# The two feed-forwards of a hybrid decoder layer: operands in a fixed order without POOL, two plain tiles, reads of products first, feeds a job sooner

## The chip, the cores and the metric

One core of a Trainium2 chip runs the whole layer as one program. The metric is the device time of the program in microseconds (us); the profile shows one execution of it, and the runs give a median. TensorE (PE) multiplies, VectorE (DVE), ScalarE (ACT) and GpSimd (POOL) work element by element, and SyncE (SP) issues the DMA transfers.

## What is computed

The reference is one layer of a decoder on 1024 tokens of width 1024, all in float32. The change touches the two feed-forwards (`D_FF` is 2816); the mixer between them and the last two lines stay.

```python
def swiglu(x, w_in, w_out):
    gate, up = jnp.split(x @ w_in, 2, axis=-1)
    return (jax.nn.silu(gate) * up) @ w_out

h = x
h = h + 0.5 * swiglu(rms_norm(h, ffn1_norm[i]), ffn1_w_in[i], ffn1_w_out[i])
h = h + hybrid_mixer(rms_norm(h, mix_norm[i]), ...)
h = h + 0.5 * swiglu(rms_norm(h, ffn2_norm[i]), ffn2_w_in[i], ffn2_w_out[i])
hn = rms_norm(h, ple_norm[i])
h = h + jax.nn.sigmoid(hn @ ple_w_gate[i]) * (p[i] @ ple_w_proj[i])
return rms_norm(h, final_norm)
```

`rms_norm(x, g)` divides by the root of the mean square and multiplies by the gain `g`. The kernel multiplies by the gain before the matmuls, and by the factor of the root, `R`, behind them.

## The kernel before

**Layout.** Activations lie transposed: eight tiles `h` of 128 channels x 1024 tokens. Each float32 operand is made of two parts for PE: ACT copies it into a rounded head, and DVE subtracts the head from the source, which leaves the rest. `part` (L282 ACT, L283 DVE) does that for an activation block of 128x512, `headrest` for a weight block, `split` for a whole 128x1024 tile. A product of two such operands takes three matmuls (head x head, head x rest, rest x head) of 512 columns.

**Seven products.** A job is one pair of output tiles times all its inputs. Both factors are cut into 2x2 blocks, and seven products of sums of blocks stand in for eight. `SEVEN = (1, 5, 6, 3, 7, 2, 4)` is the order of the products, called q = 0 to 6 in the loops. Three banks of PSUM hold them: products 1, 6, 7 and 4 add up in bank 0, 5 and 3 in bank 1, 2 has its own. A bank that takes another product must be read before that product is added to it; `done` reads it, on ACT or DVE. A job of four block pairs has 7 x 12 = 84 matmuls, one of three 63. The first job is plain, with eight products in four banks: 96 matmuls.

**Jobs.** A feed-forward has 22 jobs for the hidden layer (job 0 plain, 1 to 21 by sevens) and then 12 for the output: three windows of hidden tiles (`WINDOWS`), four jobs each (22 to 25, 26 to 29, 30 to 33; the last four are the short ones). 2784 matmuls in all.

**Operands of the hidden jobs.** `ffn` first goes through the eight tiles: square them, multiply by the gain in place (L324, DVE), make the plain blocks, and `ready` makes the sums of blocks on DVE and POOL (L308 to L311) and their parts. These are issued on engines without an order of their own: the compiler's planner orders them by simulated time. The sums of squares go to POOL and DVE (`squares`, L517, L519); the statistics are transposed on PE (`pstat`), reduced on DVE, raised to -1/2 on POOL, and spread by four matmuls with `ones` (`pr`), which ACT copies into `R`.

**Weights.** `load7` loads a job's blocks (two transfers of 512 KB, buffers `wr` for two jobs), `sums7` makes four sums on POOL (`ws`), `split7` makes the next head and rest; five buffers `w` let it run up to four products ahead (`AHEAD`). In `seven`, after the matmuls of a product:

```python
            self.split7()
            if q < 4:
                self.sums7(job + 1, q)
            if q == 3:
                self.load7()
            j.done(p, ps[at])
```

**Order.** `self.te`, `self.ve`, `self.ac` and `self.pl` (`_InOrder`) keep the instructions that go through them in the order of the program on their engine; `nc.vector` and the like are free, as are transfers on SP. `later(job, q, f)` runs `f` after product q of a job.

**Output jobs.** `hidden` gates the products and stores each hidden tile (`hid`), and `sums` stores sums of blocks of them (`ts`), with two of their four operations on POOL. For each window a `feed` loads blocks of `hid` and `ts` (256 KB each, buffers `b`, at most six asked ahead) and makes `part`s of them during the last job before the window and its first job. `bring` loads the residual tiles, two at a time (`hr`), and `added` adds the products to them. In the last window the result is squared again, and split (`take`) for the stage that follows.

Of the kernel before, what the change touches and what calls it, by code (L numbers as in the profile page):

```python
# [55 lines left out]
class Layer:  # L56
# [143 lines left out]
    def start(self, jobs):  # L200

        self.jobs = jobs
        self.loaded, self.ready, self.todo = 0, [], collections.defaultdict(list)
        self.next = (1, 0)
# [17 lines left out]
    def sums7(self, job, step):  # L222
# [10 lines left out]
        self.pl.tensor_tensor(j.w[p], x, y, op=op)  # L233
# [16 lines left out]
    def seven(self, job):  # L250
# [3 lines left out]
        for q, p in enumerate(SEVEN):  # L254
# [24 lines left out]
    def part(self, src, pool, tag, ac=None, eng=None):  # L279

        o = pool.tile([P, T], FR, tag=tag, name="xo")
        (ac or self.ac).activation(o[:, :512], src, AF.Copy)  # L282
        (eng or self.ve).tensor_tensor(o[:, 512:], src, F(o[:, :512]), op=ALU.subtract)  # L283
        return o

    def ffn(self, hs, gain, gain2, d, keep, pool, hp, xa, follow, beside=None):


        nc = self.nc
        lo, hi = slice(0, 512), slice(512, 1024)  # L290
        vx, ax, px = nc.vector, nc.scalar, nc.gpsimd
# [9 lines left out]
        plain, late = {}, []  # L301
        square, R, rs = self.squares(pool, False)

        def ready(kp):

            y1, y2 = hs[2 * kp], hs[2 * kp + 1]
            t1, t2, t3 = m(), m(), m()
            vx.tensor_tensor(t1, y1[:, hi], y1[:, lo], op=ALU.subtract)  # L308
            px.tensor_tensor(t3, y2[:, hi], y1[:, hi], op=ALU.subtract)
            vx.tensor_tensor(t2, y2[:, hi], t1, op=ALU.subtract)  # L310
            px.tensor_tensor(y2[:, lo], y2[:, lo], t2, op=ALU.subtract)  # L311
            for p, t in ((5, t1), (6, t2), (7, t3)):
                xs[p][kp] = self.part(t, *place(p), ax, vx)

            def four():
                xs[4][kp] = self.part(y2[:, lo], *place(4))
            self.later(1, kp, four)

        for kp in range(KP):
            for j in (2 * kp, 2 * kp + 1):  # L320
                square(j, hs[j])
                if keep is not None:
                    nc.sync.dma_start(keep[j], hs[j])
                vx.tensor_scalar(hs[j], hs[j], self.gains[:, gain + j:gain + j + 1], None, op0=ALU.mult)  # L324
                for p, h in (((1, lo), (0, hi)), ((2, lo), (3, hi)))[j % 2]:
                    o = plain[j, h.start] = self.part(hs[j][:, h], *place(p), ax, vx)
                    if p:
                        xs[p][kp] = o
            if kp:
                ready(kp - 1)  # L330
        ready(KP - 1)


# [9 lines left out]
        def feed(wi):  # L343
# [4 lines left out]
            for c in range(n):  # L348
                while todo and len(asked) < 6:
# [3 lines left out]
                    asked.append((t, p, i))  # L353
                t, p, i = asked.pop(0)
# [60 lines left out]
        for f in range(1, NF):  # L415
# [7 lines left out]
        w = self.jobs[0].w  # L423
        pp = {(a, h): self.psum([P, 512], F32, tag="d", name="pd") for a in range(2) for h in (0, 512)}
        for step in range(4):
            self.sums7(1, step)
        self.load7()
        self.split7()
        for kp in range(KP):
            ks = slice(kp * P, (kp + 1) * P)  # L430
            for i in range(2):
                for a in range(2):
                    for ww, halves in ((0, (0, 512)), (1, (0,))):
                        for h in (0, 512):
                            for v in halves:
                                self.te.matmul(pp[a, h], w[a + 1, i + 1][:, ww, ks], plain[2 * kp + i, h][:, v:v + 512],
                                               start=(kp == 0 and i == 0 and ww == 0 and v == 0),
                                               stop=(kp == KP - 1 and i == 1 and ww == 1))
        for _ in range(AHEAD - 1):
            self.split7()  # L440
        next(rs)
        self.later(1, 0, lambda: next(rs, None))

        def first():
            g = pool.tile([P, T], F32, tag="t", name="g")
            u = us[0] = hp.tile([P, T], F32, tag="h", name="u")
            for a, t in enumerate((g, u)):
                for h in (lo, hi):
                    self.ve.tensor_tensor(t[:, h], pp[a, h.start], R[:, h], op=ALU.mult)
            self.ac.activation(g, g, AF.Silu)  # L450
            self.ve.scalar_tensor_tensor(u, u, 0.5, g, op0=ALU.mult, op1=ALU.mult)
            nc.sync.dma_start(hid[0], u)
        self.later(1, 1, first)
# [4 lines left out]
        for job in range(1, len(self.jobs)):  # L458
# [4 lines left out]
            if out + 1 in (0, KP, 2 * KP):  # L463
                wi = (out + 1) // KP
                feeds, made, turn = feed(wi), 0, 0
                total, freed = 7 * (WINDOWS[wi][1] - WINDOWS[wi][0]), self.jobs[job].n // P
            if out == 2 * KP:
                square, Rn, rsn = self.squares(pool, True)
# [6 lines left out]
            for q in self.seven(job):  # L475
                if feeds is not None:
# [901 lines left out]
```

## Time and profile before

| what | value |
|---|---|
| median of 3 runs (lowest to highest) | 2762.5 us (2756.7 to 2762.56) |
| profiled execution | 2760.93 us |
| its span, first to last instruction | 2759.2 us |
| mean granted clock of PE | 0.975 |
| first feed-forward, then mixer, second feed-forward, end | 0 to 711, to 1928, to 2627, to 2759 us |

The profile is of one execution. Times in it count from the start of the span. An engine's busy time is the time in which it had an instruction running. A wait is given with its releaser, the work that ended last before the waiting instruction began. Matmuls overlap, so a run of them is read by its start, its length and its count.

### The profile page before, as it was taken

To read this page: it belongs to the slowest core of one execution; us is meant where nothing else is said; L and a number is where in the kernel's file an instruction comes from. 1 tells how busy PE (TensorE), PEld (TensorE's weight loads), DVE (VectorE), ACT (ScalarE), POOL (GpSimd) and SP (SyncE) were. 2 spreads that over 40 slices of the span, in tenths; PEclk is the share of its full clock that TensorE was granted. 3 is DMA by queue.
4 is the path that set the end of the run, shared out by engine and by line. 5 is a ranking of instruction groups with operands and counts; after the bars stand their busy time and mean duration, and the time that the engine had idled before them with its cause. 6 is when DMAs were issued, how large, how long until landed. Compare 5 with 4: busy or idle time off the path is not lost.

```text
span 2759.2 us, 33250 instructions
## 1 busy us (share of the span) xinstructions
PE 2598.9 (94%) x12022; PEld 2149.6 (78%) x12022; DVE 1806.6 (65%) x3138; ACT 1143.9 (41%) x1797; POOL 886.9 (32%) x599
## 2 busy tenths in 40 slices
PE   5999999999999999899999999999599999899897
PEld 3788887787788878788778877888488888788776
DVE  8555556777668999987255663232865555877776
ACT  4333334344455455523256662121443333443542
POOL 6455554422000240423222220110555555432300
PEclk9999999999999999999999999999799999999999
DMA  2243334444323233332432255332033233554322
GB/s 108 92 141 111 111 107 168 169 163 134 110 75 109 85 123 115 115 125 74 165 104 88 93 211 217 115 120 96 19 122 126 102 120 122 185 181 132 104 93 84
DMA packets 124068, 333.61 MB, mean 121 GB/s; under 512 B 13912, under 2 KB 34304, under 8 KB 123904
## 3 DMA queue, kind: packets, MB, share of 16 engines
q1 hardware_dynamic: 123904, 331.49, 34.7%
q8 instruction: 94, 1.54, 0.2%
q14 instruction: 70, 0.57, 0.1%
HBM read 226.55 MB, written 102.26 MB: 119 GB/s over the span
## 4 chain that ended last, share of the span: by engine, by line
PE 42%; DVE 4%; ACT 2%; DMA 2%; issue 1%; POOL 0%; DVEq 0%; POOLq 0%; SPq 0%; ACTq 0%
PE pd L1265 21%; PE pd L139 17%; DVE xo L283 1%; PE ptp L1195 1%; DMA b<-d_ts 1%; DMA a_l<-d_dq 0%; DVE xo L1265 0%; DVE a_l L1172 0%; DVE w L1265 0%; PE pqk L1153 0%; PE pv L1203 0%; DMA xh<-d_og 0%; PE pqk L1154 0%; PE pv L1204 0%; PE pqk L1156 0%
## 5 line engine op out<-in xcount | busy, mean ns | idle before, releaser
L1265 PE MATMUL pd<-xo,w 128*128 128x512 f32 x5568 | 1299.7, 395 | 89.2 <-DVE xo L283 34.8
L1265 PEld LDWEIGHTS pd<-xo,w 128*128 128x128 f32 x5568 | 1060.4, 191 | 327.2 <-DVE xo L283 41.1
L139 PE MATMUL pd<-xh,wh 128*128 128x512 f32 x1346 | 532.1, 397 | 12.4 <-DVE z L930 11.9
L139 PE MATMUL pd<-xl,wh 128*128 128x512 f32 x1346 | 530.9, 396 | 0.0
L139 PE MATMUL pd<-xh,wl 128*128 128x512 f32 x1346 | 453.5, 395 | 0.0
L1265 DVE TENSOR_TENSOR w<-wr,w 128x512 fp32r<-128x512 f32 (+1 forms) x272 | 231.0, 851 | 213.2 <-ACT w L1265 213.0
L139 PEld LDWEIGHTS pd<-xh,wh 128*128 128x128 f32 x1346 | 254.8, 190 | 67.4 <-DVE z L930 11.6
L139 PEld LDWEIGHTS pd<-xl,wh 128*128 128x128 f32 x1346 | 255.2, 190 | 51.9 <-issue 0.5
L139 PEld LDWEIGHTS pd<-xh,wl 128*128 128x128 f32 x1346 | 254.3, 190 | 52.9 <-issue 0.7
L118 DVE TENSOR_TENSOR wl<-wr,wh 128x1024 fp32r<-128x1024 f32 (+1 forms) x106 | 127.9, 1206 | 193.3 <-issue 96.6
L1265 ACT ACTIVATE w<-wr 128x512 fp32r<-128x512 f32 (+1 forms) x272 | 166.1, 614 | 192.7 <-PE pd L1265 140.3
L1265 POOL TENSOR_TENSOR g<-g,R 128x512 f32<-128x512 f32 x84 | 122.7, 1461 | 378.0 <-ACT g L1265 378.0
L1265 ACT ACTIVATE w<-ws 128x512 fp32r<-128x512 f32 (+1 forms) x198 | 122.4, 618 | 275.4 <-PE pd L1265 179.7
L117 ACT ACTIVATE wh<-wr 128x1024 fp32r<-128x1024 f32 (+1 forms) x106 | 101.7, 960 | 251.8 <-PE pd L139 236.0
L1265 POOL TENSOR_TENSOR ws<-wr 128x512 f32<-128x512 f32 (+1 forms) x66 | 104.5, 1583 | 249.5 <-DVE w L1265 143.0
L1265 DVE TENSOR_TENSOR hr<-hr,pd 128x512 f32<-128x512 f32 x168 | 114.8, 683 | 100.7 <-PE pd L1265 100.3
L1265 DVE TENSOR_TENSOR w<-ws,w 128x512 fp32r<-128x512 f32 (+1 forms) x198 | 138.8, 702 | 2.3 <-ACT w L1265 0.7
L1265 DVE TENSOR_TENSOR xo<-b,xo 128x512 fp32r<-128x512 f32 x154 | 124.2, 846 | 6.3 <-ACT xo L1265 6.2
L1265 ACT ACTIVATE g<-pd 128x512 f32<-128x512 f32 x84 | 50.3, 599 | 154.8 <-PE pd L1265 154.8
L999 POOL TENSOR_TENSOR g_e<-g_b 128x512 f32<-128x512 f32 x28 | 33.4, 1191 | 243.5 <-DVE g_b L973 182.2
L1265 POOL TENSOR_TENSOR ws<-wr,ws 128x512 f32<-128x512 f32 (+1 forms) x66 | 98.2, 1488 | 26.3 <-DVE w L1265 22.6
L1265 DVE TENSOR_SCALAR_CACHE_REDUCE k_junk<-sc,k_t 128x384 uint8<-128x384 f32 (+3 forms) x128 | 103.5, 809 | 3.0
(276 smaller groups left out, 3364.5 us busy)
## 6 DMA issues: line engine op xcount, KB each, us to landing
wr<-wm SPq DMA_DIRECT2D x54, 512.0 KB, 3.4
wr<-w1i SPq DMA_DIRECT2D x44, 512.0 KB, 4.1
d_hid<-u SPq DMA_DIRECT2D x44, 512.0 KB, 4.7
d_ts<-ts SPq DMA_DIRECT2D x44, 512.0 KB, 2.6
b<-d_ts SPq DMA_DIRECT2D x88, 256.0 KB, 4.0
wr<-w2i SPq DMA_DIRECT2D x44, 512.0 KB, 4.0
b<-d_hid SPq DMA_DIRECT2D x66, 256.0 KB, 4.7
wr<-w1o SPq DMA_DIRECT2D x16, 512.0 KB, 5.4
```

The source lines that it names most:

```text
L117: (ac or nc.scalar).activation(wh, raw, AF.Copy)
L118: (eng or self.weng).tensor_tensor(wl, raw, F(wh), op=ALU.subtract)
L139: te.matmul(ps[h], ww[:, ks], v[:, h * 512:h * 512 + 512], start=first and ww is wh and v is xh, stop=last and ww is wl)
L283: (eng or self.ve).tensor_tensor(o[:, 512:], src, F(o[:, :512]), op=ALU.subtract)
L999: nc.gpsimd.tensor_tensor(ev[:, :, :m], ref, bv[:, :, :m], op=ALU.subtract)
L1195: nc.tensor.transpose(pt[:, x, i, :], ls[i][:, (s + x) * P:(s + x + 1) * P], self.ident)
L1265: ins = getattr(self.eng, name)(*args, **kw)
```

## The change

In the first feed-forward jobs 0 and 1 are plain (`start(..., 2)`), in the second only job 0. All operand work goes through the ordered engines, in the order written. The gain is no longer multiplied in place: it is a scale of ACT's head and a factor in DVE's rest (`head`, `rest`). Sums of blocks are made kind by kind in `with_sums` on DVE (with ACT where a block only needs its gain), between the plain products; squares add up on DVE alone. `seven` reads a product (`done`) before it splits the next weight. In the jobs `crowded` (21 and 22) the sums of weights are made on DVE. A feed asks for its first six blocks at product 5 one job sooner and makes its parts over 13 instead of 12 products; residual tiles come two in each of jobs 21 to 24; squares of the result go into products 2 and 4 of the next job. In the first feed-forward the loads of job 1's weights stand behind x.

The core of the diff:

```diff
     def start(self, jobs, plain):
-        self.load7()
-        self.load7()
-        j = jobs[0]
-        j.w = {k: self.headrest(j.blk[k], j.n) for k in ((1, 1), (1, 2), (2, 1), (2, 2))}
+        self.load7()
+        self.blocks(0, (1, 2))
+
+    def blocks(self, f, rows):
+        j = self.jobs[f]
+        for r in rows:
+            for c in (1, 2):
+                j.w[r, c] = self.headrest(j.blk[r, c], j.n)
...
+            j.done(p, ps[at])
             self.split7()
             if q < 4:
-                self.sums7(job + 1, q)
+                self.sums7(job + 1, q, self.ve if job in self.crowded else None)
             if q == 3:
                 self.load7()
-            j.done(p, ps[at])
...
+    def head(self, src, pool, tag, gain=None):
         o = pool.tile([P, T], FR, tag=tag, name="xo")
+        if gain is None:
+            self.ac.activation(o[:, :512], src, AF.Copy)
+        else:
+            self.ac.activation(o[:, :512], src, AF.Copy, scale=gain)
         return o
+    def rest(self, o, src, gain=None):
+        if gain is None:
+            self.ve.tensor_tensor(o[:, 512:], src, F(o[:, :512]), op=ALU.subtract)
+        else:
+            self.ve.scalar_tensor_tensor(o[:, 512:], src, gain, F(o[:, :512]), op0=ALU.mult, op1=ALU.subtract)
...
+        self.crowded = (NF - 1, NF)
...
+        def tile_alone(j):
+            if keep is not None:
+                nc.sync.dma_start(keep[j], hs[j])
+            two = ((1, lo), (0, hi)) if j % 2 == 0 else ((2, lo), (3, hi))
+            os = [self.head(hs[j][:, h], *place(p), gains[j]) for p, h in two]
+            for (p, h), o in zip(two, os):
+                self.rest(o, hs[j][:, h], gains[j])
...
+        def with_sums(p, kps=range(KP)):
+            at = {}
+            for kp in kps:
+                y1, y2 = hs[2 * kp], hs[2 * kp + 1]
+                g1, g2 = gains[2 * kp:2 * kp + 2]
+                if p == 5:
+                    o, x = y1[:, lo], None
+                    self.ve.tensor_tensor(o, y1[:, hi], y1[:, lo], op=ALU.subtract)
+                    self.ac.activation(o, o, AF.Copy, scale=g1)
...
+                if x is not None:
+                    self.ve.scalar_tensor_tensor(o, x, g2, y, op0=ALU.mult, op1=ALU.subtract)
+                at[kp] = o
+                xs[p][kp] = self.head(o, *place(p))
+            for kp in kps:
+                self.rest(xs[p][kp], at[kp])
+
+        for j in range(KD):
+            tile_alone(j)
+            if plain == 1:
+                square(j, hs[j])
+        if plain > 1:
+            for j in range(KD):
+                square(j, hs[j])
+            self.blocks(1, (1,))
+            self.load7()
+        else:
+            self.load7()
+            self.sums7(plain, 0, self.ve)
+            self.split7()
+        with_sums(5)
+        if plain > 1:
+            self.blocks(1, (2,))
+            self.load7()
+        else:
+            self.sums7(plain, 1, self.ve)
+            self.sums7(plain, 2, self.ve)
+            self.split7()
...
+        if plain == 1:
+            next(rs, None)
+            with_sums(6)
+            self.sums7(plain, 3, self.ve)
+            self.split7()
+            with_sums(7)
+            self.split7()
+        else:
+            pps.append({})
+            for a, h in ((0, 0), (0, 512), (1, 0), (1, 512)):
+                if (a, h) == (1, 0):
+                    next(rs, None)
+                elif (a, h) == (0, 512):
+                    next(rs)
+                    with_sums(6)
+                elif (a, h) == (1, 512):
+                    evacuate(0)
+                pps[1][a, h] = self.psum([P, 512], F32, tag="d", name="pd")
+                for kp in range(KP):
+                    for i in range(2):
+                        matmuls(1, kp, i, a, h, kp == 0 and i == 0, kp == KP - 1 and i == 1)
...
+            with_sums(7)
+            self.sums7(plain, 3, self.ve)
+            self.split7()
+        for kp in range(KP):
+            self.later(plain, kp, lambda kp=kp: with_sums(4, (kp,)))
+        self.later(plain, 1, lambda: evacuate(plain - 1))
...
-                if feeds is not None:
+                if feeds is not None and out + 1 not in (-1, KP - 1, 2 * KP - 1):
                     turn += 1
-                    while made < min(total, -(-total * turn // 12), freed * turn):
+                    while made < min(total, -(-total * turn // 13), freed * turn):
...
-                if job == NF - 1 and q in (3, 6):
-                    bring(q // 3 - 1)
-                if job == NF and q > 4:
-                    bring(q - 3)
+                if out + 2 in (0, KP, 2 * KP) and q == 5:
+                    feeds = feed((out + 2) // KP)
+                    next(feeds)
+                if -1 <= out < KP - 1 and q == 4:
+                    bring(out + 1)
+                if out > 2 * KP and q in (2, 4):
+                    j = 2 * (out - 2 * KP - 1) + (q == 4)
+                    square(j, H[j])
+                    if j < 2:
+                        take(j)
...
         def square(j, h):
-            ss = parts[j % 2]
-            if j < 2:
-                ac.activation(ss, h, AF.Square)
+            if j == 0:
+                self.ac.activation(ss, h, AF.Square)
             else:
                 sq = self.unit(tpool, "t", "sq")
-                ac.activation(sq, h, AF.Square)
-                (ve if j > 5 else pl).tensor_tensor(ss, ss, sq, op=ALU.add)
-            if j == KD - 1:
-                ve.tensor_tensor(parts[0], parts[0], parts[1], op=ALU.add)
+                self.ac.activation(sq, h, AF.Square)
+                self.ve.tensor_tensor(ss, ss, sq, op=ALU.add)
```

## Rows read from the trace of the kernel before

**Rows 1.** Page: busy us, share of the span, instructions of each engine.

```profile
PE 2598.9 (94%) x12022; PEld 2149.6 (78%) x12022; DVE 1806.6 (65%) x3138; ACT 1143.9 (41%) x1797; POOL 886.9 (32%) x599
```

**Rows 2.** Stretches: length, busy (instructions) by engine, clock, DMA share, GB/s.

```profile
0.00:88.00 88.00, 48.42 (x156) 33.40 (x156) 65.14 (x70) 37.45 (x58) 43.64 (x25) 0.88 0.25 91
88.00:440.00 352.00, 351.98 (x1553) 291.55 (x1554) 207.10 (x284) 133.77 (x225) 191.29 (x128) 1.00 0.33 116
440.00:492.00 52.00, 43.09 (x190) 35.08 (x188) 41.74 (x50) 27.75 (x50) 29.63 (x20) 0.98 0.57 208
...
1928.60:2001.90 73.30, 44.53 (x157) 33.02 (x155) 63.62 (x64) 32.14 (x51) 41.22 (x19) 0.79 0.07 22
```

**Rows 3.** Stretches again, PE's product matmuls (`pd`) alone: length, busy (count), clock.

```profile
0.00:88.00 88.00, 44.44 (x144) 0.88 0.25 91
1928.60:2001.90 73.30, 41.75 (x145) 0.79 0.07 22
```

**Rows 4.** PE in order of time, 440 to 711: start, length, count [wait before].

```profile
439.71 34.84 PE L1265 MATMUL pd<-xo,w 128*128 128x512 f32 x153
476.64 8.45 PE L1265 MATMUL pd<-xo,w 128*128 128x512 f32 x36 [2.08 <-DVE u L1265]
491.92 78.69 PE L1265 MATMUL pd<-xo,w 128*128 128x512 f32 x336 [6.83 <-DVE hr L1265]
572.10 89.95 PE L1265 MATMUL pd<-xo,w 128*128 128x512 f32 x393 [1.49 <-DVE hr L1265]
665.05 17.29 PE L1265 MATMUL pd<-xo,w 128*128 128x512 f32 x63 [3.00 <-DVE hr L1265]
684.05 14.56 PE L1265 MATMUL pd<-xo,w 128*128 128x512 f32 x63 [1.71 <-DVE hr L1265]
700.33 10.72 PE L1265 MATMUL pd<-xo,w 128*128 128x512 f32 x45 [1.72 <-ACT xh L1265]
```

**Rows 5.** PE in order of time, 2390 to 2614.

```profile
2390.53 10.06 PE L1265 MATMUL pd<-xo,w 128*128 128x512 f32 x36 [2.08 <-DVE u L1265]
2405.77 79.21 PE L1265 MATMUL pd<-xo,w 128*128 128x512 f32 x336 [5.17 <-DVE hr L1265]
...
2580.91 16.15 PE L1265 MATMUL pd<-xo,w 128*128 128x512 f32 x63 [3.66 <-DVE hr L1265]
2598.77 14.54 PE L1265 MATMUL pd<-xo,w 128*128 128x512 f32 x63 [1.71 <-DVE hr L1265]
```

**Rows 6.** All engines in order of time, 6 to 87.

```profile
6.30 2.19 ACT L1265 ACTIVATE w<-wr 128x512 fp32r<-128x512 f32 x4 [4.29 <-DMA wr<-w1i]
...
8.18 1.80 POOL L1265 TENSOR_TENSOR ws<-wr 128x512 f32<-128x512 f32 x1 [7.74 <-DMA wr<-w1i]
...
24.63 1.28 DVE L283 TENSOR_TENSOR xo<-h,xo 128x512 fp32r<-128x512 f32 x2
...
76.20 10.69 PE L1265 MATMUL pd<-xo,w 128*128 128x512 f32 x36
```

**Rows 7.** DVE groups by line and shape, 0 to 90: busy, mean ns | idle before.

```profile
L310 DVE TENSOR_TENSOR m<-h,m 128x512 f32<-128x512 f32 x4 | 6.0, 1494 | 0.0
```

**Rows 8.** ACT and PE in order of time, start of the second feed-forward.

```profile
1928.37 0.63 ACT L1265 ACTIVATE w<-wr 128x512 fp32r<-128x512 f32 x1 [9.73 <-PE pd L139]
...
1991.46 1.12 PE L1265 MATMUL pr<-ss,ones 128*128 128x512 f32 x2 [1.25 <-ACT R L181]
```

**Rows 9.** In order of time near 484, and ACT's waits from 455 to 500.

```profile
483.88 1.73 POOL L1265 TENSOR_TENSOR ws<-wr 128x512 f32<-128x512 f32 x1
...
484.39 5.12 DVE L1265 TENSOR_TENSOR xo<-b,xo 128x512 fp32r<-128x512 f32 x3
...
ACT xo L1265 <- DMA b<-d_hid: 4.9, 4, 2.0
```

**Rows 10.** In order of time near 680: sums of squares and a weight rest.

```profile
678.12 4.77 POOL L1265 TENSOR_TENSOR ss<-ss,sq 128x1024 f32<-128x1024 f32 x2 [17.39 <-ACT sq L1265]
...
680.52 2.78 DVE L1265 TENSOR_TENSOR w<-wr,w 128x384 fp32r<-128x384 f32 x1 [1.54 <-ACT w L1265]
```

More of the change, by code (lines that the diff above doesn't have):

```diff
@@ L300, in ffn @@
         xs = {p: [None] * KP for p in SEVEN}
[L301 to L317, printed above, removed]
@@ L319, in ffn @@
-        for kp in range(KP):
-            for j in (2 * kp, 2 * kp + 1):
-                square(j, hs[j])
[L322 to L330, printed above, removed]
@@ L331, in ffn @@
-        ready(KP - 1)
+        alone = {}
+        square, R, rs = self.squares(pool)
+        gains = [self.gains[:, gain + j:gain + j + 1] for j in range(KD)]
+        def tile_alone(j):
[5 more added lines that the diff above has]
+                self.rest(o, hs[j][:, h], gains[j])
+                alone[j, h.start] = o
+                if p:
+                    xs[p][j // 2] = o
@@ L347, in feed, with ask @@
             n, asked = len(todo), []
-            for c in range(n):
+            def ask():
                 while todo and len(asked) < 6:
@@ L353, in feed @@
                     asked.append((t, p, i))
+            ask()
+            yield 0
+            for c in range(n):
+                ask()
                 t, p, i = asked.pop(0)
@@ L413, in added @@
             return done
-        for f in range(1, NF):
+        for f in range(plain, NF):
             self.jobs[f].ops = xs
@@ L439, in ffn, with matmuls @@
[L439 to L444, printed above, removed]
+        pps = []
+        def matmuls(f, kp, i, a, h, first, last):
+            w, x, ps = self.jobs[f].w[a + 1, i + 1], alone[2 * kp + i, h], pps[f][a, h]
+            ks = slice(kp * P, (kp + 1) * P)
+            for ww, v in ((0, 0), (0, 512), (1, 0)):
+                self.te.matmul(ps, w[:, ww, ks], x[:, v:v + 512], start=first and ww == 0 and v == 0,
+                               stop=last and ww == 1)
@@ L450, in first @@
             self.ac.activation(g, g, AF.Silu)
             self.ve.scalar_tensor_tensor(u, u, 0.5, g, op0=ALU.mult, op1=ALU.mult)
-            nc.sync.dma_start(hid[0], u)
-        self.later(1, 1, first)
+            nc.sync.dma_start(hid[f], u)
+            if f % 2:
+                sums(f)
+        pps.append({(a, h): self.psum([P, 512], F32, tag="d", name="pd") for a in range(2) for h in (0, 512)})
+        for kp in range(KP):
+            if kp == KP - 1 and plain == 1:
+                next(rs)
+            for a, i in ((a, i) for a in range(2) for i in range(2)) if kp == KP - 1 else \
+                    ((a, i) for i in range(2) for a in range(2)):
+                for h in (0, 512):
+                    matmuls(0, kp, i, a, h, kp == 0 and i == 0, kp == KP - 1 and i == 1)
@@ L456, in ffn @@
+        for kp in range(KP):
+            self.later(plain, kp, lambda kp=kp: with_sums(4, (kp,)))
+        self.later(plain, 1, lambda: evacuate(plain - 1))
         feeds, made, turn = None, 0, 0
         follow, raws, xn = list(follow), [], None
-        for job in range(1, len(self.jobs)):
+        for job in range(plain, len(self.jobs)):
             if job < NF:
@@ L551, in run @@
         self.first = []
-        self.start(self.products(a, "w1"))
+        self.start(self.products(a, "w1"), 2)
         hs = []
@@ L605, in run @@
         self.weng = nc.vector
-        self.start(self.products(a, "w2"))
+        self.start(self.products(a, "w2"), 1)
+        self.load7()
         pxs = []
```

73 lines of the change are left out of this document (35 added, 38 removed).

## The prediction

> **What bounds the kernel now.** The busy shares come first: TensorE (PE) is busy 94% of the 2759.2 us, DVE 65%, ACT 41%, POOL 32% [rows 1]. A PE at 94% leaves only its idle time to win, so the next view is the table of stretches [rows 2]. Between 88 and 440 us PE issues 1553 matmuls in 352 us, 0.227 us each, at a clock of 1.00: nothing to gain in steady jobs. Counting matmuls against 0.227 gives what every other stretch loses. By 88.0 us PE has done 144 product matmuls [rows 3], worth 32.7 us: 55.3 us are gone. From 1928.6 to 2001.9 us it did 145, worth 32.9 us of 73.3: 40.4 us gone. In both DVE is busy for 74% and 87% of the stretch: it makes the operands, and PE waits for it.
>
> The runs of PE show the rest [rows 4]: a wait of 2.08 and one of 6.83 us where the output products begin, and the 336 matmuls behind the long one take 78.69 instead of 76.2 us. With 0.3 us in the run of 36 that is 11.7 us. The four later waits (1.49, 3.00, 1.71, 1.72) and the runs behind them (63 matmuls in 17.29 us instead of 14.3; 0.9, 0.3 and 0.5 us in the others) lose 12.6 us more. The second feed-forward repeats both [rows 5]: 2.08 + 1.9 + 5.17 + 3.0 = 12.2 us, and at least 3.66 + 1.9 + 1.71 + 0.3 = 7.6 us late. So some 140 us of the span can be reached by these edits, and the mixer between 711 and 1928 us, which no edit touches, is taken at nothing.
>
> **What DVE pays for POOL.** Two DVE operations of 128x512 behind each other take 1.28 us [rows 6], so one comes each 0.60 us. In the first 90 us the four at L310 took 1494 ns each [rows 7], while POOL worked. Later three with POOL sums beside them took 5.12 us instead of 1.88 [rows 9]: 1.08 us lost for each. I charge 1.08 us of DVE for each POOL sum beside a full DVE. The Trainium skill (SBUF — State Buffer, section "SBUF: two separate sides") says the two engines take a shared port pair as an exclusive lock for a whole instruction; the rows agree that DVE is held, but 1.08 us is less than the 1.73 us of the POOL sum in rows 9. By the rule at its fullest, eight moved sums would be worth 8 x (1.73 - 0.60) = 9.0 us of DVE instead of the 3.8 us used below.
>
> **Start of the first feed-forward.** Two weight loads now stand behind x on SP, so the first tile of x lands where the third load did, at 8.18 us [rows 6], not fifth. ACT finishes the four weight heads at 8.49 (6.30 + 2.19, 0.55 each) and the first operand head at 9.1: PE starts there. Each tile of x then costs ACT two heads (1.1 us) and DVE two rests (1.2 us), nothing else; PE needs 12 matmuls, 2.7 us, for it, and becomes the slowest. Gains are folded into the operand operations, so eight L324 operations go. Squares follow (seven sums of 1024 columns, some 1.2 us each, end near 28 us by this pace, before the statistics need them).
>
> PE: 9.1, plus 192 matmuls x 0.227 = 43.6, plus 2.5 for the slow first run (36 matmuls after a wait took 10.69 instead of 8.2 us, rows 6), plus some 6 for statistics (pairs of 1.12 us with 1.25 us between them [rows 8], and the transposes with their reductions), plus 1 for the second half of the first operand: 62 us. DVE has, up to the last product of job 2, about 100 operations x 0.60 = 60 us from 9 us on, plus 6 to 8 us where it waits on ACT, which waits for weight buffers that the last quarter of job 0 frees: 76. PE wants that product at 62 + 6 x 2.7 = 78, so DVE is just in time; I add 2.5 us. Effectively 192 matmuls at 64.6, where before stood 144 at 88.0. The extra plain job costs 96 instead of 84, so 2604 matmuls remain instead of 2640: 36 x 0.227 = 8.2. Gain 23.4 + 8.2 = 31.6; I take 30 (24 with 7 us more of DVE waiting, 35 with none).
>
> **Start of the second.** The heads are ordered behind the fourth weight, which waits for a buffer until 1928.37 us [rows 8], so nothing is made earlier and the first product matmuls (1928.6 before) come near 1931. DVE is the bound: until the last product of job 1 it has 66 operations of 512 columns (16 rests, 4 weight sums, 7 weight rests, 32 for four kinds of operands, 4 evacuations, 3 sums into gate and up) = 39.6 us, nine of 1024 = 10.8, 2 us of reductions, 1.2 us of the mixer's last sums: 54 us, plus 4 x 1.08 for POOL's sums of job 2's weights, plus some 2 us of waits (estimate): 1989. That product then ends at 1992 with 180 matmuls done; before 180 stood at 2001.9 + 35 x 0.227 = 2009.8. Gain 18 (8 if the reductions queue behind operand sums and PE stands, 26 if PE alone set it: 1931 + 38.1 + 6 + 2.7 = 1978 to 1984).
>
> **Output products begin.** Jobs 21 and 22 need, on DVE, 60 operations plus POOL's toll before: 36 us + about 11 x 1.08 = 48 us, where PE has 38 us of work. The change takes eight weight sums from POOL to DVE: 4.8 us more of work, 8.6 less of toll: 44 us. The feed asks six transfers at product 5 of job 20 (SP holds nothing that needs these buffers), so the 4.9 us of ACT waiting for d_hid blocks [rows 9] shrink at its start; later asks still wait for a buffer and hold SP's queue. The four pairs of residual loads move one to a job (jobs 21 to 24), so fewer fall together; the first has three products, 8.2 us, to land. Reading a product ahead of the next weight split shortens PE's wait for the bank; the split comes up to a product (2.7 us) later, hidden by the three weights still ready (8.2 us). I take half of 11.7 and of 12.2: 12 us for both (2 if only the toll's 3.8 net counts in part, 20 if the stalls go).
>
> **Late jobs.** At 678.12 us POOL's two square sums take 4.77 us, and the weight rest of DVE beside them 2.78 us instead of some 0.6, with the read of a product queued behind it [rows 10]. Sums of squares go to DVE, 1.2 us each, two to a job of 14.3 us in which DVE has about 8 us (seven weight rests, seven reads); the first two splits of the result no longer stand in one lump after a job. I take 7 of 12.6 us and 6 of at least 7.6: 13 (5 to 20).
>
> **Sum.** 30 + 18 + 12 + 13 = 73 us from the profiled execution's 2760.9 us gives 2688; the median of the runs is 1.6 us higher, so **2689 us**. With all lower ends (39) 2723, with all upper (101) 2661.
>
> **Rivals.**
> - *DVE is overfull where the output begins* (chance 20%). It has 44 us of work for 38. If the toll stays for the remaining POOL sums and parts still wait for DMA, those 12 us become a loss of 5: 2706. For it: DVE busy 41.74 of 52 us [rows 2]. Against: the toll of rows 9.
> - *The fixed order blocks at the starts* (15%). One waiting weight head on ACT holds every operand behind it, and a reduction stands behind operand sums while PE waits. First start 22, second 8: 2707. For it: rows 8. Against: in the first start PE is the slowest.
> - *POOL's toll is larger* (10%). If each moved operation frees the whole 1.73 us of rows 9 and the late waits go altogether, crowded and late parts give 20 each: 2674, down to 2661 with both starts at their best. The skill's lock rule (SBUF — State Buffer, "SBUF: two separate sides") points this way.
> - *Slower* (5%). The split of each weight behind the read: if it reached PE in steady jobs, 455 products (32 and 33 jobs of seven) would each pay. From 73 / 455 = 0.16 us a product on, all is given back; at 0.25 us, 2689 + 114 = 2803. Against: ACT 0.55 and DVE 0.60 us in 8.2 us of lead, and DVE at 207 of 352 us.
> - *No change* (2%): the gains of the starts return as waits in the next jobs, because DVE enters them behind. Then 2762. Against: after 88 us DVE is 59% busy and catches up.
>
> **How the numbers follow.** The forecast as summed holds 48%, its own range 2674 to 2704. The first two rivals lie above, with the lower ends at 2723, the third below; 2662 to 2726 leaves out the last two rivals and their neighbours. A measurement here tells 0.2%, 5.5 us, from no change. Faster 0.93, same 0.02, slower 0.05.
>
> **What will show it.** Right: the first product matmul near 9 us; job 0 of the first feed-forward without waits over 1 us; 192 product matmuls by about 62 us; L324 gone; DVE operations of 512 columns near 0.68 us in both starts; last product of job 1 in the second start waiting for DVE; no 6.83 us wait near 490 us; late waits below 1 us. Wrong: ACT idle on a weight buffer for more than 3 us in the first start, POOL sums still beside slow DVE operations, waits of PE in the steady stretch (fewer than 1553 matmuls in 352 us), or residual loads that land after the read which needs them.

## The result, and the profile after

The changed kernel takes **2730.72 us** (median of 4 runs, 2728.41 to 2732.71); beside it the kernel before took 2762.39. The ratio is 0.989, with a 95% interval of 0.9873 to 0.9907: 31.7 us less. The prediction had the sign, and 2689 us with a range of 2662 to 2726; it forecast 73 us of gain.

The profiled span went from 2759.2 to 2730.9 us. Counting product matmuls backwards from the last one of each feed-forward puts it on the prediction's terms: the last 564 are the late jobs, the 372 before them are where the output products begin, and all ahead of them is the start with its steady jobs. "Mixer" is what lies between the two feed-forwards. Each row adds up to the span (us), one profiled execution each:

```
                 start 1  begin  late | mixer | start 2  begin  late |  end  | span
before             474.4   96.1 140.4 |1217.7 |  459.7    96.5 141.9 | 132.5 | 2759.2
changed            457.2   97.9 136.7 |1222.1 |  446.6    96.3 140.5 | 133.7 | 2730.9
gain (measured)     17.2   -1.8   3.7 |  -4.4 |   13.1     0.2   1.4 |  -1.2 |   28.3
gain (forecast)       30    12 (both) |     0 |     18    late: 13 (both)    |   73
```

So no term was right in size, and the 25 us of the output jobs came to 3.5. The mixer, which no edit touches, took 1215.9 to 1222.1 us over all the profiles below; why it varies was not followed up, and a single span can't be read closer than that.

The stretches of the changed kernel, with the columns of [rows 2]:

```profile
0.00:88.00 88.00, 69.50 (x274) 54.66 (x275) 64.33 (x89) 48.34 (x72) 10.35 (x10) 0.96 0.33 124
88.00:440.00 352.00, 347.53 (x1524) 287.24 (x1523) 211.45 (x282) 124.96 (x221) 187.63 (x128) 0.99 0.33 114
```

In the first 88 us PE has 69.50 us of work where it had 48.42. That the second stretch has 1524 matmuls and not 1553 comes from waits before 98 us: behind them 1584 matmuls take 359 us, 0.227 us each as before. Jobs 21 and 22 of the first feed-forward, from their first matmul to the first of job 23, in the kernel before and in the changed one:

```profile
458.07:507.89 49.82, 40.91 (x169) 33.04 (x168) 45.53 (x59) 26.59 (x47) 22.07 (x14) 0.93 0.73 260
440.92:491.47 50.55, 41.96 (x169) 32.61 (x168) 47.12 (x67) 25.89 (x48) 11.72 (x7) 0.95 0.77 271
```

POOL fell from 22.07 to 11.72 us, as the edit says, but DVE rose from 45.53 to 47.12, and the two jobs take no less time than before.

PE in order of time in the first start (start, length, count, wait before):

```profile
9.73 0.79 PE L1353 MATMUL pd<-xo,w 128*128 128x512 f32 x1 [9.73 <-ACT xo L1353]
10.75 29.68 PE L1353 MATMUL pd<-xo,w 128*128 128x512 f32 x119 [0.23 <-DVE xo L1353]
...
44.17 6.86 PE L1353 MATMUL pd<-xo,w 128*128 128x512 f32 x24
...
53.13 16.90 PE L1353 MATMUL pd<-xo,w 128*128 128x512 f32 x72
71.31 3.02 PE L1353 MATMUL pd<-xo,w 128*128 128x512 f32 x12 [1.28 <-ACT g L1353]
76.92 4.61 PE L1353 MATMUL pd<-xo,w 128*128 128x512 f32 x12 [2.59 <-ACT u L1353]
82.99 5.76 PE L1353 MATMUL pd<-xo,w 128*128 128x512 f32 x24 [1.45 <-ACT g L1353]
93.22 32.12 PE L1353 MATMUL pd<-xo,w 128*128 128x512 f32 x131 [4.47 <-DVE u L1353]
```

The two plain tiles go nearly as forecast: first matmul at 9.73 us, 120 matmuls with no wait over 0.3 us, 24 between the steps of the statistics, and 72 more without a wait. Of these 72 the first 48 belong to the plain tiles, whose 192nd matmul ends at 64.6 us where about 62 was forecast, and the last 24 to job 2. Then come four waits of 9.8 us in all inside job 2, where the prediction had put 2.5. Three of them are for ACT to read a product (g, u). What ACT does just before:

```profile
63.97 0.71 ACT L1353 ACTIVATE h<-h,gains 128x512 f32<-128x512 f32 x1
65.50 0.63 ACT L1353 ACTIVATE xo<-h 128x512 fp32r<-128x512 f32 x1 [0.82 <-DVE h L1353]
66.03 0.71 ACT L1353 ACTIVATE h<-h,gains 128x512 f32<-128x512 f32 x1
67.56 0.63 ACT L1353 ACTIVATE xo<-h 128x512 fp32r<-128x512 f32 x1 [0.82 <-DVE h L1353]
...
70.68 0.58 ACT L1353 ACTIVATE g<-pd 128x512 f32<-128x512 f32 x1
```

`with_sums(7)` goes scale on ACT, sum on DVE, head on ACT, scale on ACT, and so on. Each pair costs a round trip of 2.06 us (63.97 to 66.03) instead of the 1.3 us of work on ACT, and the read of job 2's first product, the last row, stands behind four of them in ACT's fixed order. In the second start PE's longest wait is for the same read (there job 1's), behind four such pairs:

```profile
1960.42 7.82 PE L1353 MATMUL pd<-xo,w 128*128 128x512 f32 x24 [5.73 <-ACT g L1353]
```

PE where the output begins and in the late jobs, against [rows 4]:

```profile
469.84 11.62 PE L1353 MATMUL pd<-xo,w 128*128 128x512 f32 x43 [2.31 <-DVE hr L1353]
481.77 1.76 PE L1353 MATMUL pd<-xo,w 128*128 128x512 f32 x6 [0.31 <-DVE xo L1353]
484.78 1.66 PE L1353 MATMUL pd<-xo,w 128*128 128x512 f32 x6 [1.25 <-DVE xo L1353]
488.75 0.97 PE L1353 MATMUL pd<-xo,w 128*128 128x512 f32 x3 [2.31 <-DVE xo L1353]
490.45 64.87 PE L1353 MATMUL pd<-xo,w 128*128 128x512 f32 x278 [0.72 <-DVE xo L1353]
...
573.01 0.96 PE L1353 MATMUL pd<-xo,w 128*128 128x512 f32 x3 [0.84 <-DVE xo L1353]
574.70 70.56 PE L1353 MATMUL pd<-xo,w 128*128 128x512 f32 x309 [0.73 <-DVE xo L1353]
645.62 1.67 PE L1353 MATMUL pd<-xo,w 128*128 128x512 f32 x6 [0.36 <-DVE xo L1353]
648.12 43.83 PE L1353 MATMUL pd<-xo,w 128*128 128x512 f32 x191 [0.83 <-DVE xo L1353]
```

The 6.83 us wait for a residual half (hr) has shrunk to 2.31 (469.84). Beside it stand waits that [rows 4] does not have at all: for `xo`, an operand's rest, eight in the first feed-forward (7.4 us), nine in the second (7.8 us). They come once a window, in the last two products of the window's first job. DVE and POOL ahead of the longest, in order of time:

```profile
484.05 1.28 DVE L1353 TENSOR_TENSOR xo<-b,xo 128x512 fp32r<-128x512 f32 x2
484.20 2.27 POOL L1353 TENSOR_TENSOR ts<-u,ts 128x512 f32<-128x512 f32 x1 [16.86 <-DVE ts L1353]
485.25 0.68 DVE L1353 TENSOR_TENSOR hr<-hr,pd 128x512 f32<-128x512 f32 x1
485.85 1.18 DVE L1353 TENSOR_TENSOR w<-ws,w 128x512 fp32r<-128x512 f32 x1
486.44 1.71 POOL L1353 TENSOR_TENSOR ws<-wr 128x512 f32<-128x512 f32 x1
486.95 3.44 DVE L1353 TENSOR_TENSOR xo<-b,xo 128x512 fp32r<-128x512 f32 x2
488.23 1.62 POOL L1353 TENSOR_TENSOR ws<-ws,wr 128x512 f32<-128x512 f32 x1
```

The last two parts of the window stand behind the read of the sixth product (hr) and a weight split, and beside POOL's sums they take 3.44 us. The two before took 1.28 though POOL was at work there too: there POOL's sum was slow, 2.27 us where the same sum took 1.28 with 12 turns (at 484.92).

### The profile page after: what moved, and what is told of

It is laid out like the page before. It is cut to its first block, busy times and chain, and to the rows that moved or that the text cites. A ratio compares the mean times of both kernels' runs of the same rounds, so it can differ in the third digit from the quotient of the medians.

```text
span 2730.9 us, 33223 instructions
## 1 busy us (share of the span) xinstructions
PE 2602.3 (95%) x12034; PEld 2151.4 (79%) x12034; DVE 1798.2 (66%) x3173; ACT 1138.6 (42%) x1806; POOL 760.8 (28%) x537
## 4 chain that ended last, share of the span: by engine, by line
PE 70%; DVE 14%; issue 8%; ACT 3%; DMA 2%; POOL 1%; DVEq 0%; POOLq 0%; SPq 0%; ACTq 0%
PE pd L1353 40%; PE pd L139 22%; DVE xo L1353 2%; DVE k_junk L1353 2%; PE pq L1097 1%; DVE w L1353 1%; DVE wl L118 1%; PE ptp L1283 1%; DVE k_t L1353 1%; DVE z L1018 1%; DVE hr L1353 1%; PE psc L852 1%; PE psc L854 1%; DMA a_l<-d_dq 0%; DMA g_X<-d_r 0%
## 5 line engine op out<-in xcount | busy, mean ns | idle before, releaser
L1353 DVE TENSOR_TENSOR w<-wr,w 128x512 fp32r<-128x512 f32 (+1 forms) x272 | 207.4, 764 | 206.1 <-ACT w L1353 205.9
L1353 DVE TENSOR_TENSOR w<-ws,w 128x512 fp32r<-128x512 f32 (+1 forms) x195 | 172.3, 884 | 0.6
L1353 POOL TENSOR_TENSOR ws<-wr 128x512 f32<-128x512 f32 (+1 forms) x59 | 97.5, 1652 | 208.9 <-DVE w L1353 208.9
L1353 ACT ACTIVATE g<-g 128x512 f32<-128x512 f32 (+1 forms) x85 | 55.0, 647 | 238.0 <-DVE g L1353 238.0
L171 POOL TENSOR_TENSOR r<-r,mhalf 128x8 f32<-128x8 f32 (+1 forms) x11 | 17.0, 1541 | 372.5 <-DVE r L170 364.0
```

The costliest lines, as they stand in the source:

```text
L171: nc.gpsimd.tensor_tensor(r, r, self.mhalf[:, :nb], op=ALU.pow)
L1353: ins = getattr(self.eng, name)(*args, **kw)
```

## The experiments

The ratio behind each result is to the kernel before, with its 95% interval; the changed kernel has 0.989. "Changed kernel" without a number is 2730.7. Beside the different runs the kernel before took 2758.4 to 2762.4 us, so less than some 4 us between two medians is not read as a difference.

**The scales of the fourth sum first.**

```diff
+            if p == 7:
+                for kp in kps:
+                    self.ac.activation(hs[2*kp][:, hi], hs[2*kp][:, hi], AF.Copy, scale=gains[2*kp])
             for kp in kps:
...
                 elif p == 7:
-                    self.ac.activation(o, o, AF.Copy, scale=g1)
```

> The four ACT scales of kind 7 stand ahead of its four DVE sums and heads, nothing else changes. Theory A (the read of the first seven-product stands on ACT behind kind 7, whose scale, sum and head alternate between ACT and DVE at 2.06 us a pair): kind 7 takes some 5 us instead of 8.2, the waits for the first read (1.28 us at 71 us, 5.73 us at 1960 us) shrink by about 3 us each, and the kernel is 4 to 7 us faster than 2730.9. Rival (DVE's amount of work sets those waits): the sums come no earlier in total, within 1.5 us of no change in both starts.

2722.33 us, 0.9863 [0.9848, 0.9878]. Start 1 fell by 4.8 and start 2 by 3.2 us. The round trip of ACT and DVE costs that much, a little more than theory A expected.

**The fourth sum right behind the third** (first feed-forward).

```diff
                     next(rs)
                     with_sums(6)
+                    with_sums(7)
...
             self.split7()
-            with_sums(7)
```

> In the first feed-forward kind 7 is made right behind kind 6, while ACT (8.5 us) and DVE (some 5 us) idle for the statistics; the second feed-forward is as it was. Theory A: the stalls of job 2 (1.28, 2.59, 1.45, 4.47 us and the slow clock behind them, 14 us in all against an unbroken run) lose at least half, 7 to 10 us faster, all of it before 120 us. Rival (POOL's sums beside a full DVE make the stalls of job 2): the work is done anyway, and the gain stays under 3 us.

2724.54 us, 0.9868 [0.9852, 0.9885]. Start 1 fell by 7.2 us, start 2 stayed at 446.6. Of PE's waits in job 2 those of 1.66 and 4.50 us remain; the last one is for DVE's read of a product (u).

**The sums of the crowded jobs back on POOL.**

```diff
-        self.crowded = (NF - 1, NF)
+        self.crowded = ()
```

> Jobs 21 and 22 make the weight sums on POOL again, the rest of the change stays. The stretch where the output begins takes 98.1 us in the changed kernel and 96.1 before (first feed-forward), 96.4 and 96.5 (second). Theory B (a moved sum costs DVE 0.60 us and frees about 0.34): 2 us faster in each feed-forward. The prediction's price (1.08 us freed for each): 3.8 us slower in each.

2731.48 us, 0.9899 [0.9884, 0.9913]: no change in the median. "Begin" rose by 1.0 and 3.6 us and late 1 by 1.6; start 1, the mixer and late 2 were shorter by 2.9, 3.2 and 1.3 us.

**The splits ahead of the reads again.**

```diff
-            j.done(p, ps[at])
             self.split7()
...
                 self.load7()
+            j.done(p, ps[at])
```

> A product is read behind the next weight split again, the rest of the change stays. If reading first is worth what the prediction gave it, the crowded and late stretches get 3 to 8 us longer over both feed-forwards, through reads that come late; steady jobs stay at 0.227 us a matmul. Rival: the three weights ready ahead make the order without effect, all stretches within 1 us; or the split in the shadow of a product helps where DVE is full, and the crowded stretch gets 1 to 4 us shorter.

2715.11 us, 0.9836 [0.982, 0.9852]. Late fell by 4.4 and 7.0 us, begin by 3.2 in the first feed-forward and rose by 1.6 in the second. Reading first does shorten PE's wait for hr in job 22 (2.31 us, 3.64 with the splits first), but lengthens those for `xo` (7.4 and 7.8 us, 5.0 and 6.8 with the splits first): on balance it costs. That the late jobs gain most was in none of the expectations.

**One plain tile in the first feed-forward too.**

```diff
-        self.start(self.products(a, "w1"), 2)
+        self.start(self.products(a, "w1"), 1)
```

> The first feed-forward starts like the second, with one plain job, 12 matmuls (2.7 us) fewer in all. Theory: the second start is held by DVE and by the read behind kind 7, and lost 12 us more than two plain jobs would have had by PE alone; the first start then takes 3 to 9 us longer than the 457.2 us of the changed kernel (less the 2.7 us saved), the rest is unchanged. Rival: the plain job only puts off the same queue on ACT and DVE, and the start is 2 to 4 us shorter by the saved matmuls.

2728.63 us, 0.9893 [0.9878, 0.9908]. Start 1 is 455.7 against 457.2: the second plain tile brings nothing, and the theory (3 to 9 us longer without it) missed. What start 1 gained comes with the other edits there (the order, the gains folded in, the sums and squares taken from POOL), which no run separates.

**The old feed.** 12 turns, begun with the window, no early loads, residual loads in their old places.

```diff
-                if feeds is not None and out + 1 not in (-1, KP - 1, 2 * KP - 1):
+                if feeds is not None:
...
-                    while made < min(total, -(-total * turn // 13), freed * turn):
+                    while made < min(total, -(-total * turn // 12), freed * turn):
...
-                if out + 2 in (0, KP, 2 * KP) and q == 5:
-                    feeds = feed((out + 2) // KP)
-                    next(feeds)
-                if -1 <= out < KP - 1 and q == 4:
-                    bring(out + 1)
+                if job == NF - 1 and q in (3, 6):
+                    bring(q // 3 - 1)
+                if job == NF and q > 4:
+                    bring(q - 3)
```

> Feeds begin with their window again, over 12 products, and residual tiles are loaded as before; all else as in the changed kernel. Theory B (the crowded stretch is held by DVE's work, not by the blocks' arrival): the stretch where the output begins stays within 2 us of 97.9 and 96.3 us, the late stretches too. Rival (late blocks): 3 to 6 us longer in each feed-forward, with longer waits of ACT for blocks of d_hid and d_ts.

2708.67 us, 0.9818 [0.9804, 0.9833]. Both expectations missed: the new feed costs 22 us. Begin and late fell by 5.3, 4.9, 3.7 and 5.6 us.

**Reading first alone**, put into the kernel before:

```diff
+            j.done(p, ps[at])
             self.split7()
...
-            j.done(p, ps[at])
```

> The kernel before with one edit: a product is read ahead of the next weight split. Theory R (a DVE that is full in a stretch stands idle at each read until PE has ended the product, with the split queued behind it): the crowded and late stretches of both feed-forwards get 8 to 16 us longer in all, steady jobs do not change, so 0.3 to 0.6% slower than the kernel before. Rival (reading first only pays with POOL out of the way or not at all): within 3 us.

2755.84 us, 0.9991 [0.9981, 1.0]: nothing. What the splits ahead of the reads gave in the changed kernel is thus not a price of reading first by itself, but of reading first with something else of the change.

**Scales first, fourth sum early and splits first together.**

> The changed kernel with the four scales of kind 7 first, kind 7 right behind kind 6 in the first start, and the split ahead of the read. If the three effects add (about 7 us in the first start, 3 in the second, 11 in the crowded and late stretches, up to 4 in the mixer by another planner's order): 2706 to 2713 median. If they overlap in the same waits of DVE: 2713 to 2720.

2709.95 us, 0.9826 [0.9812, 0.9841], less than the sum of the three (30 us). Start 1 is 454.5, worse than with either edit of the sums alone. PE shows why:

```profile
52.56 2.05 PE L1356 MATMUL pr<-ss,ones 128*128 128x512 f32 x2 [4.88 <-DVE ss L174]
55.30 2.08 PE L1356 MATMUL pr<-ss,ones 128*128 128x512 f32 x2 [0.69 <-ACT R L181]
56.38 30.13 PE L1356 MATMUL pd<-xo,w 128*128 128x512 f32 x120
```

With both edits DVE has the fourth sum's operands in front of the statistics; PE waits 4.88 us for `ss`, and the two `pr` matmuls behind take 2.05 us where they took 1.02 in the changed kernel.

The old feed had three parts; the next three runs each put one of them back. **12 turns alone:**

```diff
-                    while made < min(total, -(-total * turn // 13), freed * turn):
+                    while made < min(total, -(-total * turn // 12), freed * turn):
```

> The changed kernel with the parts of a window made over 12 products again, not 13; the early six loads and the moved residual loads stay. Putting the whole feed back gave 2708.7, 22 us less than the changed kernel. Theory T (the thirteenth turn: every operand's split is queued up to a twelfth later, so that the split that a product needs stands in DVE's full queue right in front of it, which shows as PE waits for xo in 481 to 490, 573 and 648): this one edit gives most of it back, 2709 to 2716, in the early and the late output products of both feed-forwards alike. Theory H (the residual loads, moved into the stretch where the DMA engines are 0.81 busy, ahead of the parts' loads): within 3 us of 2730.7.

2711.8 us, 0.9828 [0.9813, 0.9842]: one constant gives back 18.9 of the 22 us. Of the 19.7 us between the two profiled spans 15.5 lie in the stretches of the output jobs and 3.3 in the mixer. PE in the same stretches as above:

```profile
469.95 6.01 PE L1353 MATMUL pd<-xo,w 128*128 128x512 f32 x24 [0.79 <-ACT w L1353]
476.56 5.69 PE L1353 MATMUL pd<-xo,w 128*128 128x512 f32 x24 [0.60 <-DVE hr L1353]
483.79 1.87 PE L1353 MATMUL pd<-xo,w 128*128 128x512 f32 x7 [1.53 <-DVE hr L1353]
486.80 0.96 PE L1353 MATMUL pd<-xo,w 128*128 128x512 f32 x3 [1.15 <-DVE xo L1353]
488.49 63.30 PE L1353 MATMUL pd<-xo,w 128*128 128x512 f32 x278 [0.72 <-DVE xo L1353]
553.87 76.70 PE L1353 MATMUL pd<-xo,w 128*128 128x512 f32 x330 [2.08 <-DVE hr L1353]
631.21 8.50 PE L1353 MATMUL pd<-xo,w 128*128 128x512 f32 x36 [0.63 <-ACT w L1353]
```

The waits for `xo` fell from 7.4 to 1.9 us in the first feed-forward and from 7.8 to none in the second. Begin is now 94.9 and 92.6, late 133.5 and 134.9.

**The old places of the residual loads alone** (the `bring` lines of the old feed):

> The changed kernel with the four pairs of residual loads back in their old places (two pairs in the last hidden job, two at the end of the first output job); 13 turns and the early six loads stay. Theory H: the pairs no longer stand ahead of the parts' loads in the full stretch, the wait of ACT for a part (5.3 us at 483.7) goes, and 5 to 12 us come back, all of it where output begins: 2719 to 2726. Theory T: within 3 us of 2730.7. If PE's waits for the residual halves themselves are what counts, it is slower than 2731.

2729.65 us, 0.9898 [0.9881, 0.9914]: nothing. Theory H falls.

**Without the early loads** (the feed begins with the window; 13 turns):

> The changed kernel without the early six loads (they go out with the first part of the window, as before); 13 turns and the moved residual loads stay. Both theories T and H say that this alone changes nothing to the good: 2728 to 2736. The prediction's assumption that the early loads save waits for a part's data says slower, 2733 to 2740. A theory L (the early six take the buffers that the sums of the job before need, and make the queue of SP stand) says faster, 2710 to 2722.

2729.65 us, 0.9893 [0.9878, 0.9908]: the six early loads bring and cost nothing.

**Old feed, scales first, fourth sum early, splits first:**

> The old feed, the splits ahead of the reads, the scales first and the fourth sum early, together; order, plain tiles and sums on DVE as in the changed kernel. The old feed alone is 2708.7, the splits first alone 2715.1, the three others together 2710.0. If reading first and the new feed cost by the same mechanism (DVE's queue standing in front of a split that PE needs), the two savings overlap: 2698 to 2706. If they are two separate costs, they add: 2684 to 2694.

2701.37 us, 0.9789 [0.9775, 0.9804]: the savings overlap. It has the wait at the statistics too (3.49 us), and its DVE shows what stands in front of the statistics (L169, L170, L174):

```profile
45.13 0.68 DVE L169 TENSOR_REDUCE r<-pstat 128x4 f32<-128x512 f32 x1
45.74 2.07 DVE L1353 SCALAR_TENSOR_TENSOR h<-h,gains,h 128x512 f32<-128x512 f32 x3
47.72 0.16 DVE L170 TENSOR_SCALAR r<-r 128x8 f32<-128x8 f32 x1
47.79 2.49 DVE L1353 TENSOR_TENSOR xo<-h,xo 128x512 fp32r<-128x512 f32 x4
51.82 1.22 DVE L174 TENSOR_TENSOR ss<-ident,r 128x1024 f32<-128x1024 f32 x1 [1.54 <-POOL r L171]
```

**11 turns:**

```diff
-                    while made < min(total, -(-total * turn // 13), freed * turn):
+                    while made < min(total, -(-total * turn // 11), freed * turn):
```

> The changed kernel with the parts of a window made over 11 products. 13 gave 2730.7, 12 gave 2711.8. Theory D (deadline: at 13 the last part is queued right behind the last product but one, and DVE is one product behind PE; at 12 one product of slack hides that): at 11 only the waits left at 12 can go, 1.9 us of PE's waits for xo in the first feed-forward, and 2706 to 2712 is expected. Theory S (a plain slope: DVE's work in the output jobs counts, and each turn fewer moves it out): as much again as from 13 to 12, 2692 to 2700. If the hidden job, which has to take the parts, is the tighter one: 2714 to 2722.

2711.62 us, 0.982 [0.9805, 0.9834]: no waits for `xo` are left, and the time is that of 12 turns. It is a deadline, not a slope.

**12 turns, sums on POOL** (`crowded` empty):

> The changed kernel with 12 turns and with the operand sums of the two crowded jobs back on POOL. By the prediction's pricing (1.08 us of DVE's time freed for each sum moved, less the 0.6 that it costs there), undoing the move costs 3.8 us a feed-forward, 7 to 8 in all: 2718 to 2721. By the toll read from the changed kernel's splits (0.34 us for each moved sum), the move loses DVE time, and undoing it gains 1 to 4: 2707 to 2711. If POOL's sums come later than DVE's and the wait for ws decides, it is slower by more: over 2722.

2714.33 us, 0.9829 [0.9814, 0.9844], against 0.9828 with the sums on DVE: the medians tell no difference. Jobs 21 and 22 of both feed-forwards, with the columns of [rows 2], first 12 turns with the sums on DVE, then with them on POOL:

```profile
440.43:489.06 48.63, 41.55 (x169) 32.14 (x168) 45.98 (x67) 26.81 (x48) 9.13 (x6) 0.96 0.75 262
2334.16:2380.48 46.32, 41.16 (x169) 32.20 (x168) 43.97 (x67) 26.77 (x48) 8.00 (x5) 0.96 0.77 259
```

```profile
439.03:489.24 50.21, 42.93 (x170) 34.50 (x168) 46.35 (x59) 26.38 (x48) 22.11 (x14) 0.90 0.67 239
2333.90:2384.15 50.25, 42.42 (x169) 34.20 (x168) 46.29 (x59) 26.30 (x48) 21.88 (x14) 0.90 0.67 235
```

With the sums on DVE it has eight operations more, 4.8 us at 0.60 each, and yet is busy for 0.4 and 2.3 us less. So the eight and nine operations that POOL has less free 5.2 and 7.1 us of DVE, 0.65 and 0.8 us each. The two jobs are 1.6 and 3.9 us shorter with the sums on DVE, the late stretches 1.7 and 1.6 us longer. The time lies between the two expectations: undoing the move neither costs 7 nor gains 1.

**12 turns, scales first, splits first:**

> The changed kernel with 12 turns, the scales of the fourth sum first, and the splits ahead of the reads. With 12 turns alone 2711.8. The scales first gave 8.4, in stages that 12 turns do not touch, so they add: 2703. The splits first gave 15.6 with 13 turns; if that was the same wait for a part (theory T), little is left, 0 to 8: 2695 to 2703. If it is separate, 2688.

2698.37 us, 0.9776 [0.976, 0.9793], the fastest, 32 us under the changed kernel. Its late jobs, the second row, are one run of 564 matmuls without a wait between them:

```profile
465.38 78.86 PE L1356 MATMUL pd<-xo,w 128*128 128x512 f32 x336 [3.75 <-DVE hr L1356]
545.74 128.76 PE L1356 MATMUL pd<-xo,w 128*128 128x512 f32 x564 [1.49 <-DVE hr L1356]
```

## Why the prediction was wrong, step by step

**The step that failed: the feed.** The paragraph on the output products costed its early loads, its residual loads and its queue, but not the line that makes the parts over 13 products instead of 12: that stood at nothing. The working would have been a count. Parts are made behind the read of a product, in DVE's fixed order. A window has 28 (the last one 21); the last product of its first job needs all of them. At 13 turns 26 are made behind the read of its fifth product (28 x 12 / 13, rounded up) and the last two behind the read of the sixth. That read cannot come before the sixth product ends, and six matmuls (1.4 us) into the seventh PE turns to its third block pair, whose part DVE has still to make behind the read and a weight split: the row of 3 matmuls behind 2.31 us at 488.75. The waits of 0.84 us at 573.01 and 0.83 at 648.12 stand at the same place of the other two windows. At 12 turns all 28 are made behind the fifth read, a product (2.7 us) sooner. Runs with 13, 12 and 11 turns gave 2730.7, 2711.8 and 2711.6: one turn of slack is all that there is to gain. The 15.5 us of it in the output jobs are about a third of the 44.7 us by which the profiled span missed the forecast (73 less 28.3). The two starts, below, make 17.7 us of it in two terms.

**Late jobs, 13.** Measured 5.1; with 12 turns 6.9 + 7.0 = 13.9. This fits the mechanism forecast, sums of squares on DVE (1.22 us each, 1.2 forecast) and no lump on POOL: the 191 matmuls from 648.12 us on run without a wait, where [rows 4] have 3.00, 1.71 and 1.72 us. The thirteenth turn lay over it. No run puts the squares back alone, so that part is argued.

**Output products begin, 12.** Measured -1.6; with 12 turns 1.2 + 3.9 = 5.1. In the rest the toll was mis-sized: 1.08 us for each POOL sum was one row [rows 9], among the worst; over jobs 21 and 22 it is 0.65 to 0.8 us, hardly more than the 0.60 that a sum costs on DVE. So moving the sums frees 0.4 and 2.3 us of DVE, not 3.8 in each feed-forward. The first rival, DVE overfull, was right in that DVE stays the limit there (47.12 of 50.55 us), but gave parts that wait for their loads as the cause, and the two runs on the loads changed nothing (2729.65 us both). The third rival, a larger toll, had it the wrong way round. The Trainium skill (SBUF — State Buffer, section "SBUF: two separate sides") has the port pair locked for the whole instruction; by that rule at its fullest a moved sum would free the 1.73 us of [rows 9], and the trace disagrees as to the size: 0.65 to 0.8 us.

**Reading first.** The prediction took it as a help. With the splits first again the changed kernel gains 15.6 us, and with 12 turns and the scales first about 5 (2711.8 less the scales' 8.4 is 2703.4; measured 2698.4); the kernel before loses nothing by reading first. Read with the count above, a part of its price is that of the deadline: with the read first, the weight's split stands between the read and the parts that PE waits for. The stretches of the output jobs in the profiles say the same: the splits first take 12.9 us off them with 13 turns, 7.8 with 12, and nothing with the whole old feed (451.9 against 452.2 us), in pairs that differ otherwise in the starts at most. What the 7.8 us are is open, and that it is this order and no other effect was argued, not isolated.

**Start of the first, 30.** Measured 17.2. The lane of PE was nearly right (first matmul 9.73 against 9.1 us, the 192nd done at 64.6 against 62, with no waits but at the statistics). The 2.5 us for DVE "just in time" failed: the 84 matmuls behind the 192nd took 33.7 us instead of 19.1, by 9.8 us of waits and slower matmuls behind them. The prediction added up each engine's operations and left out the chain between two of them. The two runs on it give back 4.8 and 7.2 us. The 8.2 us of the sum only count that more matmuls are done by then; that one plain tile would be as fast, the prediction did not consider.

**Start of the second, 18.** Measured 13.1, 16.3 with the scales first; the same chain (5.73 us at 1960.42). The second rival, a fixed order that blocks at the starts (22 and 8 us), saw the mechanism, with its weight on the other start.

**Mixer, 0.** It took 4.4 us more in this profile, within its spread.

**The rival "slower".** The split behind the read did not reach the steady jobs (0.227 us a matmul, as before), so nothing went towards slower.

Open: 3.75 and 1.49 us of waits for residual halves at the first jobs of two windows in the fastest version, and why the mixer varies by 6 us.

## What to carry to other kernels

Where one in-order engine both reads a product and makes what a later product needs, count, turn by turn, what is made behind which read: a schedule that ends one turn before its use stalls at every window, and a constant in it can outweigh all the edits around it. A sum of operations for each engine is a lower bound only; where two engines hand a tile back and forth, add the round trip, or let one of them run through all its part first. Price contention by the same jobs with and without it, not by the row that looks worst.

## What the runs showed of the hardware

Where DVE and POOL work side by side, either can be the slow one: two DVE operations took 3.44 us instead of 1.28 at 486.95 us in the changed kernel, and just before, at 484.20, it was the POOL sum (2.27 us instead of 1.28) and DVE lost nothing. Over two whole jobs a POOL sum costs a busy DVE 0.65 to 0.8 us. A wait costs more than itself: behind the 4.88 us for the statistics two `pr` matmuls take 2.05 us instead of 1.02, and the granted clock of the stretch is 0.83 against 0.94 in the changed kernel: more of it at 1.2 GHz, the lower level, and less at 2.4. Here are both stretches, the changed kernel's first, then the version with scales, fourth sum and splits:

```profile
40.00:70.00 30.00, 26.78 (x110) 20.72 (x109) 19.61 (x29) 12.57 (x19) 4.94 (x3) 0.94 0.13 45
```

```profile
40.00:70.00 30.00, 22.86 (x81) 16.55 (x82) 20.08 (x30) 12.31 (x19) 7.11 (x3) 0.83 0.10 39
```
